# Out projection stage of a hybrid backbone layer: direction sums accumulated in PSUM, second norm on ScalarE, routing by pairs of tiles

## The chip, the cores and the metric

One NeuronCore of a Trainium2 chip runs the whole layer in one launch. The metric is device time in microseconds of one execution. PE is the matrix engine (TensorE), DVE is VectorE, ACT is ScalarE, POOL is GpSimd, and SP is the engine whose queue starts most transfers. SBUF is the on-chip memory of 128 partitions; PSUM holds the matmuls' results in eight banks, of which ACT and DVE read.

## What is computed

The reference is one layer over 2048 latent tokens of width 1024 and 256 tokens of context. An input projection feeds three mixers that run over the sequence in both directions (SSD, RWKV-7, GLA). Their normed outputs are concatenated, projected, added to the residual and normed; a second norm gives the input of a mixture of 64 experts, top 8, with one shared expert. In the part that the change touches, for each token:

```
y_ssd  = rmsnorm_groups((fwd + flip(bwd) + D*xs) * silu(z), ssd_norm_w)
y_rwkv = (groupnorm(fwd + flip(bwd)) * lnx_w + lnx_b + bonus) * gate
y_gla  = rmsnorm_groups(fwd + flip(bwd), gla_norm_w) * silu(og)
mix = concat([y_ssd, y_rwkv, y_gla]) @ w_out
x = layernorm(DN_ALPHA * x + g1 * mix, ln1_w, ln1_b)
h = layernorm(x) * (1.0 + sc2) + sh2
scores = sigmoid(h @ router_w)
sel = scores + router_b
top_g = top_k(sum of the best two sel of each of 8 groups, 4)
idx = top_k(sel where the group is in top_g, 8)
wts = scores[idx] / sum(scores[idx]) * 2.5
x = layernorm(DN_ALPHA * x + g2 * moe(h, idx, wts), ln2_w, ln2_b)
```

## The kernel before

The stage around the change is a loop over 16 tiles of 128 latent tokens, c from 17 down to 2 (the GLA and SSD backward scans take their last steps in it), between the scans and the experts:

```
for c in range(17,1,-1):
    ym=mid.mix(c,pm,y17 if c==17 else X.pass2(c),G.pass2(c))
    f=mid.proj(c,pm,mp,ym)
    rt.tile(c,mp,f,mid.rw)
```

X.pass2 (lines 906 to 920) finishes the SSD: two matmuls of the carried state with the loaded C (L916) into one PSUM bank, on DVE the decay product (L918), the sum with the forward part sy (L919), and the two steps of the next state hb (L903, L904). G.pass2 (L1111 to L1119) does the same for GLA: one matmul (L1117), one add of the forward part on DVE (L1118), one state step (L1108). mix (L1176 to L1213) turns the RWKV backward rows around with a matmul by the reversal matrix (L1189), adds the forward rows on DVE (L1190), takes sums and squares per head on ACT (L1193, L1197, L1198, L1200), a Newton rsqrt of ten columns on DVE (the helper of L35 to L44), scales on ACT (L1207 to L1209), and leaves the concatenated tile ym of 128 x 1024 (L1210 to L1212).

proj (L1231 to L1262) transposes ym by eight matmuls with the identity (L1237) and splits it into a high and a low part (yTh on ACT L1239, yTl on DVE L1240). Two groups of 24 matmuls of 128 x 512 (L1248: high by high, high by low, low by high) give the projection; each group ends in a DVE residual with row sums (L1249). The first norm `ln` (square on ACT L1220, affine steps on DVE L1221 and L1230, ten one-column DVE steps between) gives x; the second, with perm=True, gives the hidden tile m_h with its columns reordered (DVE L1221 and L1229). m_h is stored (L1254), transposed by eight matmuls into the banks a0 and a1 (L1258), copied by ACT (hTf, L1259) and stored (L1260).

rt.tile (L1281 to L1322) does the routing of one tile: eight router matmuls (L1287), exp on ACT (L1288), some 25 small DVE instructions for sigmoid, group limit, top 8 and weights, a matmul with a triangle U and one with ones that give each token's rank within its expert (L1312), and the slots (L1313 to L1322). rt.scatter later issues 128 indirect transfers on POOL (L1328) that enter tokens into the experts' lists.

PSUM tiles have names, and a name has a fixed number of buffers: `g` and `mm` two each, c0, c1, a0 and a1 one each. With one buffer, the next user of a name waits, in program order, until the last reader of the one before is done. Before the change c0 serves X.pass2, G.pass2 and mix, c1 the router and the ranks, a0 and a1 the hidden transposes. The order of instructions on each engine is set when the program is built, by a scheduler that moves instructions ahead of others as far as data and buffers allow; an engine then works through its list in order. The loads and stores of the stage all go through SP's queue.

Behind the loop come the experts: the shared expert on the first 8 tiles (up matmuls L1512), the scatter, then the routed experts.

Of the kernel before, what the change touches and what calls it, by code (L numbers as in the profile page):

```python
# [1127 lines left out]
class Mid:  # L1128
# [50 lines left out]
    def mix(s, c, pool, ys, yg):  # L1179

        nc=s.nc; l=c-2; S=s.S; r0=l*128
        ld=lambda n,src,w: (lambda t:(nc.sync.dma_start(t,src),t)[1])(pool.tile([128,w],F32,name=n,bufs=2))
# [4 lines left out]
        ym=pool.tile([128,1024],F32,name='m_ym',bufs=2)
        p=s.ps.tile([128,256],F32,name='c0',bufs=1)
        nc.tensor.matmul(p,S['rev'],yb,start=True,stop=True)  # L1189
        nc.vector.tensor_tensor(yf,p,yf,op=OP.add)  # L1190
# [6 lines left out]
        for h in range(4): nc.scalar.activation(yr[:,h*64:h*64+64],yf[:,h*64:h*64+64],AF.Square,bias=nm[:,h:h+1],accum_out=st[:,2+h:3+h])  # L1197
# [66 lines left out]
class Route:  # L1264
# [14 lines left out]
        nc.sync.dma_start(S['tab'].rearrange("(p s) c->p (s c)",p=128),tb)  # L1279
        s.slot=f([128,16,8],'q_slot',I32); s.tk=f([128,16],'q_tk',I32)  # L1280
    def tile(s, c, pool, f, rw):  # L1281
        nc=s.nc; r0=(c-2)*128
# [8 lines left out]
        sel=t([128,8,8],'sel'); sf=sel.rearrange("p a b->p (a b)")
        nc.vector.tensor_tensor(sf,sc,s.rb,op=OP.add)
        top=t([128,8,8],'top')
        for g in range(8): nc.vector.max(top[:,g],sel[:,g])
        gs=t([128,8],'gs'); nc.vector.tensor_tensor(gs,top[:,:,0],top[:,:,1],op=OP.add)
# [12 lines left out]
        w=t([128,64],'w'); nc.vector.tensor_scalar(w,sc,n,2.5,op0=OP.mult,op1=OP.mult)
        nc.sync.dma_start(s.S['h'][r0:r0+128,1024:1088],w)

        q=p[:,128:256]
        nc.tensor.matmul(q,s.U,two(M),start=True,stop=False); nc.tensor.matmul(q,s.on,two(s.cum),start=False,stop=True)  # L1312
        sl=t([128,64],'sl'); nc.vector.tensor_tensor(sl,p[:,128:192],s.e0,op=OP.add)  # L1313
# [544 lines left out]
```

## Time and profile before

| | |
|---|---|
| median of 3 runs | 3917.51 us (3916.85 to 3926.28) |
| the profiled execution | 3949.18 us, its span 3947.4 us |
| granted PE clock over the span | 0.943 |
| PE busy | 3525.1 us, 89% of the span |
| DVE busy | 2685.3 us, 68% |
| ACT busy | 1706.2 us, 43% |
| POOL busy | 1329.0 us, 34% |
| DMA | 745.81 MB, mean 189 GB/s |
| 1600 to 1900 us (end of the scans): PE, DVE, ACT busy | 227.62, 207.66, 133.19 of 300 us, clock 0.83 |
| 1900 to 2260 us (the tile stage) | 312.54, 319.08, 193.26 of 360 us, clock 0.94 |
| 2260 to 3947 us (the experts) | 1574.80, 1080.30, 603.65 of 1687 us, clock 0.97 |

Busy time is the time in which an engine executes instructions, so an engine that waits within its list is not busy. The granted clock is the TensorE clock as a share of full speed. A table by stage says more than the page's shares of the whole span, because the stages have different limits.

### The profile page before, as it was taken

Reading aid. Unit: us, or ns where it says so; the run is one execution under the profiler, and the core shown is the slowest. Engines: PE = TensorE matmul, PEld = TensorE weight load, DVE = VectorE, ACT = ScalarE, POOL = GpSimd, SP = SyncE. Lnnn points to the kernel's source line nnn. Section 1 sums busy time; section 2 is a strip of 40 time slices with the busy share of each in tenths; the row PEclk is TensorE's granted clock in tenths of the full one; section 3 lists DMA queues with packets and bytes.
Section 4 is the critical chain, followed back from the end, with each engine's and each line's share of the span. In section 5 each row is a group of like instructions: output and inputs, shape, how many; then the busy total and the mean of one; then the engine's idle time right before and its main releaser. Section 6 shows DMA issues by size and latency. Waiting matters only on the chain. (4 is left out here: it accounts for less than half of the span.)

```text
span 3947.4 us, 66654 instructions
## 1 busy us (share of the span) xinstructions
PE 3525.1 (89%) x23502; PEld 3006.8 (76%) x23502; DVE 2685.3 (68%) x6775; ACT 1706.2 (43%) x3955; POOL 1329.0 (34%) x1224
## 2 busy tenths in 40 slices
PE   8989887999799978995789899999999999999986
PEld 5978777888688857774567678888888887787865
DVE  4576865876777648775899766666666665666658
ACT  3555553545454533444555323343333333333334
POOL 0243543443343310100044533333334343344323
PEclk9999989999899988996899899999999999999988
DMA  7656554333333276864665468788788887888874
GB/s 228 212 184 206 175 152 133 83 100 101 111 92 98 51 223 215 250 186 167 199 194 167 156 172 231 220 251 243 219 241 242 251 235 227 245 242 229 254 210 160
DMA packets 498511, 745.81 MB, mean 189 GB/s; under 512 B 156704, under 2 KB 393312, under 8 KB 469216
## 3 DMA queue, kind: packets, MB, share of 16 engines
q1 hardware_dynamic: 438880, 522.20, 41.0%
q0 software_dynamic: 59296, 219.33, 22.0%
q8 instruction: 187, 3.06, 0.3%
q14 instruction: 148, 1.21, 0.1%
HBM read 524.31 MB, written 217.06 MB: 188 GB/s over the span
## 5 line engine op out<-in xcount | busy, mean ns | idle before, releaser
L1546 POOL DMA_INDIRECT d_f<-yo,en x162 | 346.6, 2140 | 569.4 <-DVE yo L1543 314.0
L1543 DVE SCALAR_TENSOR_TENSOR yo<-mm,f_w,g2r 128x512 f32<-128x512 f32 (+7 forms) x324 | 236.6, 744 | 265.6 <-PE mm L1541 171.2
L1562 POOL DMA_INDIRECT xg<-d_h,en x162 | 232.1, 1433 | 371.8 <-DVE yo L1543 61.6
L184 PE MATMUL b<-uh,wh 128*128 128x384 f32 (+1 forms) x912 | 320.1, 356 | 12.6 <-ACT sce L805 5.2
L184 PE MATMUL b<-ul,wh 128*128 128x384 f32 (+1 forms) x912 | 320.3, 352 | 5.9 <-DMA ul<-d_ul 3.6
L184 PE MATMUL b<-uh,wl 128*128 128x384 f32 (+1 forms) x912 | 320.9, 352 | 0.0
L1445 DVE TENSOR_TENSOR w13l<-raw,w13h 128x2048 fp32r<-128x2048 f32 x102 | 232.8, 2283 | 25.3 <-ACT w13h L1445 25.3
L1445 ACT ACTIVATE w13h<-raw 128x2048 fp32r<-128x2048 f32 x102 | 195.0, 1914 | 104.5 <-DMA raw<-in_exp_w_dram 94.4
L1328 POOL DMA_INDIRECT d_tab<-q_tk,q_slot x128 | 146.9, 1148 | 248.2 <-DVE q_slot L1321 135.7
L1541 PE MATMUL mm<-w2h,hWh 128*128 128x512 f32 (+7 forms) x480 | 202.3, 422 | 13.0 <-DVE yo L1543 12.3
L1512 PE MATMUL a<-w13h,xTh 128*128 128x512 f32 x464 | 190.2, 410 | 9.0 <-ACT xTh L1471 8.4
L1445 DVE TENSOR_TENSOR w2l<-raw,w2h 128x2048 fp32r<-128x2048 f32 x66 | 151.3, 2293 | 68.9 <-ACT w2h L1445 66.0
L1512 PE MATMUL a<-w13l,xTh 128*128 128x512 f32 x464 | 190.4, 410 | 8.0 <-DVE w13l L1445 8.0
L1541 PE MATMUL mm<-w2h,hWl 128*128 128x512 f32 (+7 forms) x480 | 186.9, 404 | 6.8 <-DVE hWl L1504 6.8
L1541 PE MATMUL mm<-w2l,hWh 128*128 128x512 f32 (+7 forms) x480 | 191.2, 399 | 1.6 <-DVE w2l L1445 1.6
L184 PEld LDWEIGHTS b<-uh,wh 128*128 128x128 f32 x912 | 175.9, 194 | 20.2 <-ACT sce L805 6.4
L1512 PE MATMUL a<-w13h,xTl 128*128 128x512 f32 x464 | 187.7, 405 | 0.0
L184 PEld LDWEIGHTS b<-ul,wh 128*128 128x128 f32 x912 | 177.7, 195 | 9.3 <-DVE ul L139 4.0
L184 PEld LDWEIGHTS b<-uh,wl 128*128 128x128 f32 x912 | 177.6, 195 | 1.4
L1445 ACT ACTIVATE w2h<-raw 128x2048 fp32r<-128x2048 f32 x66 | 126.5, 1916 | 116.1 <-DMA raw<-in_exp_w_dram 70.5
L1475 PE MATMUL g<-ident,xg 128*128 128x128 f32 (+9 forms) x1296 | 167.6, 263 | 9.9 <-DMA xg<-d_h,en 5.8
L1475 PEld LDWEIGHTS g<-ident,xg 128*128 128x128 f32 (+9 forms) x1296 | 142.4, 140 | 38.2 <-issue 14.6
(706 smaller groups left out, 10553.8 us busy)
## 6 DMA issues: line engine op xcount, KB each, us to landing
raw<-in_exp_w_dram SPq DMA_DIRECT2D x162, 1024.0 KB
w13h<-in_exp_w_dram SPq DMA_DIRECT2D x30, 1024.0 KB
wr<-in_w_in_dram SPq DMA_DIRECT2D x46, 512.0 KB
uht<-d_uh POOLq DMA_DIRECT2D x32, 512.0 KB
ult<-d_ul POOLq DMA_DIRECT2D x32, 512.0 KB
mrw<-in_ada_w_dram SPq DMA_DIRECT2D x32, 512.0 KB
rkX<-d_ops SPq DMA_DIRECT2D x36, 384.0 KB
rpx<-d_rw SPq DMA_DIRECT2D x54, 192.0 KB
```

The lines of the kernel that those rows point to most:

```text
L184: s.nc.tensor.matmul(P.rearrange("p (i t)->p i t",t=128),l,r[:,a//128:,k],start=(i==0),stop=(i==23)); i+=1
L1328: d=s.nc.gpsimd.indirect_dma_start(out=s.S['tab'],out_offset=bass.IndirectOffsetOnAxis(ap=s.slot[:,l,k:k+1],axis=0),in_=s.tk[:,l:l+1],in_o ...
L1445: pin(nc.scalar.activation(H,r,AF.Copy)); pin(nc.vector.tensor_tensor(L,r,rnd(H),op=OP.subtract))
L1475: for k in range(4): nc.tensor.transpose(p[:,k,:m],B['x'][:m,(4*g+k)*128:(4*g+k+1)*128],s.id[:m,:m])
L1512: nc.tensor.matmul(p,a[:,k],b[:,:,k],start=(i==0),stop=(i==23)); i+=1
L1541: nc.tensor.matmul(r[:m],a[:,k],b[:,k,cs],start=(i==0),stop=(i==5)); i+=1
L1543: else: nc.vector.scalar_tensor_tensor(o[:m,cs],r[:m],B['w'] if isinstance(B['w'],float) else B['w'][:m],s.g2[:m,cs],op0=OP.mult,op1=OP.mult)
L1546: d=nc.gpsimd.indirect_dma_start(out=s.S['f'],out_offset=bass.IndirectOffsetOnAxis(ap=B['en'][:m],axis=0),in_=o[:m],in_offset=None,compute ...
L1562: s.nc.gpsimd.indirect_dma_start(out=x[:m],out_offset=None,in_=s.S['h'],in_offset=bass.IndirectOffsetOnAxis(ap=B['en'][:m],axis=0))
```

## The change

Four edits, all in the stage described. (1) The forward parts of GLA and RWKV are no longer added on DVE: a second matmul with the identity accumulates them in PSUM, and ACT reads the sums from there. The bank that G.pass2 hands to mix (now c1) and mix's own (c0) are therefore held until the scalings at mix's end. (2) In the second norm the two wide DVE steps, one of them with reordered output, are replaced by one small DVE product, one ACT pass that normalises and reorders, and two wide DVE steps on contiguous rows; the modulation rows are reordered once, ahead of the stage. (3) Routing handles two tiles at a time: an odd tile only leaves its exp in half of a shared buffer, and the even tile after it runs the chain for both. (4) PSUM names move: X.pass2 writes a1 (before c0), G.pass2 c1 (before c0), the router a0 and the ranks a0 and a1 (before c1).

```diff
@@ G.pass2 @@
-        po=s.ps.tile([128,256],F32,name='c0',bufs=1)
-        nc.tensor.matmul(po,qb,Sb,start=True,stop=True)
-        nc.vector.tensor_tensor(y,po,y,op=OP.add)
-        return y
+        po=s.ps.tile([128,256],F32,name='c1',bufs=1)
+        nc.tensor.matmul(po,qb,Sb,start=True,stop=False)
+        nc.tensor.matmul(po,s.id,y,start=False,stop=True)
+        return po
@@ modrow @@
+        t=rowb(s.nc,pool,s.S['mod'][1024*v:1024*v+1024],1024,'mtmp' if perm else name)
+        if not perm: return t
+        o=pool.tile([128,1024],F32,name=name)
+        s.nc.scalar.activation(o.rearrange("t (k p)->t k p",k=8),t.rearrange("t (p k)->t k p",k=8),AF.Copy); return o
@@ mix @@
-        nc.tensor.matmul(p,S['rev'],yb,start=True,stop=True)
-        nc.vector.tensor_tensor(yf,p,yf,op=OP.add)
+        nc.tensor.matmul(p,S['rev'],yb,start=True,stop=False)
+        nc.tensor.matmul(p,s.id,yf,start=False,stop=True)
...
-        for h in range(4): nc.scalar.activation(yr[:,h*64:h*64+64],yf[:,h*64:h*64+64],AF.Copy,accum_out=nm[:,h:h+1])
+        for h in range(4): nc.scalar.activation(yr[:,h*64:h*64+64],p[:,h*64:h*64+64],AF.Copy,accum_out=nm[:,h:h+1])
...
-        for h in range(4): nc.scalar.activation(yf[:,h*64:h*64+64],yf[:,h*64:h*64+64],AF.Identity,bias=nb[:,h:h+1],scale=rs[:,2+h:3+h])
+        for h in range(4): nc.scalar.activation(yf[:,h*64:h*64+64],p[:,h*64:h*64+64],AF.Identity,bias=nb[:,h:h+1],scale=rs[:,2+h:3+h])
...
-        for h in range(4): nc.scalar.activation(yg[:,h*64:h*64+64],yg[:,h*64:h*64+64],AF.Copy,scale=rs[:,6+h:7+h])
-        nc.vector.tensor_tensor(ym[:,768:1024],yg,og,op=OP.mult)
+        for h in range(4): nc.scalar.activation(ym[:,768+h*64:832+h*64],yg[:,h*64:h*64+64],AF.Copy,scale=rs[:,6+h:7+h])
+        nc.vector.tensor_tensor(ym[:,768:1024],ym[:,768:1024],og,op=OP.mult)
@@ ln @@
-        nc.vector.scalar_tensor_tensor(u,x,ve[:,0:1],w,op0=OP.add,op1=OP.mult)
+        if not perm: nc.vector.scalar_tensor_tensor(u,x,ve[:,0:1],w,op0=OP.add,op1=OP.mult)
...
-            nc.vector.scalar_tensor_tensor(o,v(u),rs,v(b),op0=OP.mult,op1=OP.add)
+            nc.vector.tensor_tensor(ve[:,0:1],ve[:,0:1],rs,op=OP.mult)
+            nc.scalar.activation(u.rearrange("t (k p)->t k p",k=8),x.rearrange("t (p k)->t k p",k=8),AF.Identity,bias=ve[:,0:1],scale=rs)
+            nc.vector.tensor_tensor(u,u,w,op=OP.mult); nc.vector.tensor_tensor(out,u,b,op=OP.add)
@@ Route.tile @@
-        p=s.ps.tile([128,512],F32,name='c1',bufs=1)
+        p=s.ps.tile([128,128],F32,name='a0',bufs=1)
...
+        if l%2: s.sc=t([128,2,64],'sc')
+        sc=s.sc; nc.scalar.activation(sc[:,l%2],p[:,0:64],AF.Exp,scale=-1.0)
+        if l%2: return
...
+        for j in (1,0):
+            q=s.ps.tile([128,128],F32,name=f'a{1-j}',bufs=1)
+            nc.tensor.matmul(q,s.U,two(M[:,j]),start=True,stop=False); nc.tensor.matmul(q,s.on,two(s.cum),start=False,stop=bool(j))
+            if not j: nc.tensor.matmul(q,s.on,two(M[:,1]),start=False,stop=True)
+            nc.vector.tensor_tensor(sl[:,j],q[:,0:64],s.e0,op=OP.add)
...
@@ the stage @@
-                X.ps=G.ps=ps; X.bank='c0'; G.pool=tp.enter_context(P('p2g',side='right'))
+                X.ps=G.ps=ps; X.bank='a1'; G.pool=tp.enter_context(P('p2g',side='right'))
-                mid.sh2=mid.modrow(mw,1,'sh2r'); mid.sc2=mid.modrow(mw,2,'sc2r')
+                mid.sh2=mid.modrow(mw,1,'sh2r',True); mid.sc2=mid.modrow(mw,2,'sc2r',True)
```

The lines of the changed kernel stand some 3 to 15 further down: L1248 is L1251 there, L1258 is L1261, L1287 is L1291.

The order of instructions moves on PE. In these rows `mm` is the projection's PSUM tile, `a_..` a0 or a1, `c_..` c0 or c1, `g` the transposes of ym, and x4 stands for four equal instructions. Before, around the hidden transposes of tile 13, the fifth of the loop:

```order
L1248 MATMUL mm<-woh,yTl 128x512
L1117 MATMUL c_22893<-gSb_20326,gq_22889 128x256
L1258 MATMUL a_21997<-ident,m_h 128x128 x4
L1258 MATMUL a_22003<-ident,m_h 128x128 x4
L1189 MATMUL c_22909<-m_yb,rev 128x256
L1312 MATMUL c_21742<-q_M,q_U 128x128
L1312 MATMUL c_21742<-q_cum,q_on 128x128
L916 MATMUL c_23148<-hb_20316,sC_23144 128x256 x2
L1287 MATMUL c_22010<-rtw,hTf 128x128 x8
L1117 MATMUL c_23161<-gSb_20327,gq_23157 128x256
L1189 MATMUL c_23177<-m_yb,rev 128x256
L1237 MATMUL g<-ident,m_ym 128x128 x8
```

These stand behind the projection matmuls of seven tiles (17 to 11): two more than its own and those ahead of it. After, around the hidden transposes of tile 15:

```order
L1251 MATMUL mm<-woh,yTl 128x512
L1261 MATMUL a_21446<-ident,m_h 128x128 x4
L1261 MATMUL a_21452<-ident,m_h 128x128 x4
L1291 MATMUL a_21459<-rtw,hTf 128x128 x8
L916 MATMUL a_21478<-hb_20316,sC_21474 128x256 x2
L1192 MATMUL c_21799<-m_yb,rev 128x256
L1193 MATMUL c_21799<-m_yf,ident 128x256
L1117 MATMUL c_21783<-gSb_20326,gq_21779 128x256
L1118 MATMUL c_21783<-gy_21781,ident 128x256
L1240 MATMUL g<-ident,m_ym 128x128 x8
L1251 MATMUL mm<-woh,yTh 128x512
L1251 MATMUL mm<-wol,yTh 128x512
```

They stand behind the matmuls of three tiles, 17 to 15: the last set in front of them is the tile's own, and the next set (14's) comes behind the router, X.pass2 and the sums. So it is in all 16 tiles.

On ACT, before, where copies of one tile (yTh), statistics of a second and third, and norm passes of others alternate:

```order
L1239 ACTIVATE yTh<-g 128x512 x2
L1198 ACTIVATE m_ym,m_st<-gy_22355 128x64 x4
L1200 ACTIVATE m_z,m_st<-so_22347 128x256 x2
L1193 ACTIVATE m_ym,m_nm<-m_yf 128x64 x4
L1197 ACTIVATE m_ym,m_st<-m_yf,m_nm 128x64 x4
L1208 ACTIVATE m_ym<-so_22079,m_rsy 128x256 x2
L1209 ACTIVATE gy_22087<-gy_22087,m_rsy 128x64 x3
L1220 ACTIVATE m_h,l2e<-m_x,l2e 128x1024
L1207 ACTIVATE m_yf<-m_yf,m_nb,m_rsy 128x64 x4
L1209 ACTIVATE gy_22087<-gy_22087,m_rsy 128x64
L1239 ACTIVATE yTh<-g 128x512 x2
L1220 ACTIVATE m_h,l1e<-m_xt,l1e 128x1024
```

These are pieces of at least three tiles. After, around the norms of tile 15:

```order
L1242 ACTIVATE yTh<-g 128x512 x2
L1223 ACTIVATE m_h,l1e<-m_xt,l1e 128x1024
L1223 ACTIVATE m_h,l2e<-m_x,l2e 128x1024
L1231 ACTIVATE m_xt<-m_x,l2e,l2y 128x1024
L1262 ACTIVATE hTf<-a_21446 128x512
L1262 ACTIVATE hTf<-a_21452 128x512
L1293 ACTIVATE q_sc<-a_21459 128x64
L1203 ACTIVATE m_z,m_st<-so_21481 128x256 x2
L1211 ACTIVATE m_ym<-so_21481,m_rsy 128x256 x2
L1212 ACTIVATE m_ym<-c_21491,m_rsy 128x64 x3
L1210 ACTIVATE m_yf<-c_21507,m_nb,m_rsy 128x64 x4
L1212 ACTIVATE m_ym<-c_21491,m_rsy 128x64
```

The two norm squares (L1223), the reordering pass (L1231), the hidden copies (L1262) and the exp (L1293) of one tile now follow each other, then the mix of the next tile (L1203 to L1212).

On SP, before, around the two stores of a tile's hidden state (d_h, d_hT):

```order
L1254 DMA d_h<-m_h 128x1024
L1114 DMA gq_23961<-gqb 128x128
L1107 DMA gbs<-gstb 128x256
L1260 DMA d_hT<-hTf 128x1024
L1182 DMA m_yb<-d_yb 128x256
L911 DMA sC_24216<-ssdC 128x2x128
```

Two loads of later GLA steps stand between the stores, and the load of C (sC) is one of several behind them. After, around the same stores of tile 15:

```order
L1257 DMA d_h<-m_h 128x1024
L1263 DMA d_hT<-hTf 128x1024
L911 DMA sC_22504<-ssdC 128x2x128
L913 DMA sy_22506<-d_ys 128x512
L902 DMA sbs<-stb 128x512
```

The loads that X.pass2 and the mix of the next tile need (sC, sy, sbs, m_z) now stand directly behind the store d_hT.

## Rows read from the trace of the kernel before

**Rows 1.** Windows ahead of and in the tile stage: stretch, length, engines' busy us, PEclk, DMA share, GB/s
```profile
1880.00:1904.00 24.00, 13.43 (x29) 7.58 (x30) 15.91 (x63) 14.74 (x80) 0.00 (x0) 0.50 0.92 288
1904.00:2210.00 306.00, 272.68 (x1360) 224.96 (x1360) 279.62 (x1276) 172.61 (x661) 111.23 (x96) 0.96 0.54 172
```

**Rows 2.** Timeline of TensorE: start us, us, instruction, [idle before it <-releaser]
```profile
1884.88 2.07 PE L916 MATMUL c<-hb,sC 128*128 128x256 f32 x4 [0.52 <-DVE m_yf L1190]
...
1903.34 0.99 PE L1248 MATMUL mm<-woh,yTh 128*128 128x512 f32 x1
...
1905.81 0.39 PE L1248 MATMUL mm<-woh,yTh 128*128 128x512 f32 x1
...
1915.37 0.40 PE L1248 MATMUL mm<-woh,yTl 128*128 128x512 f32 x1
1915.61 1.03 PE L1237 MATMUL g<-ident,m_ym 128*128 128x128 f32 x8
...
2225.21 3.78 PE L1287 MATMUL c<-rtw,hTf 128*128 128x128 f32 x16 [0.32 <-issue]
2229.74 1.94 PE L1258 MATMUL a<-ident,m_h 128*128 128x128 f32 x8 [0.74 <-DVE q_r L1316]
...
2256.18 0.38 PE L1312 MATMUL c<-q_M,q_U 128*128 128x128 f32 x2
```

**Rows 3.** Groups by line, 1870 to 2262: xcount | busy us, mean ns | idle before, releaser
```profile
L1229 DVE SCALAR_TENSOR_TENSOR m_h<-m_xt,l2y,sh2r 128x1024 f32<-128x1024 f32 x16 | 32.5, 2033 | 0.4 <-DVE q_M L1304 0.3
...
L1197 ACT ACTIVATE m_ym<-m_yf,m_nm 128x64 f32<-128x64 f32 x64 | 21.5, 338 | 15.3 <-DVE m_nm L1194 12.8 <-DVE gy L1118 1.6 <-DVE q_sl L1314 0.5
...
L1221 DVE SCALAR_TENSOR_TENSOR m_xt<-m_x,l2e,sc2r 128x1024 f32<-128x1024 f32 x16 | 20.3, 1271 | 0.0
...
L1198 ACT ACTIVATE m_ym<-gy 128x64 f32<-128x64 f32 x64 | 15.6, 247 | 24.2 <-DVE gy L1118 14.2 <-DMA m_yb<-d_yb 9.6 <-DVE m_rst L39 0.4
...
L1118 DVE TENSOR_TENSOR gy<-c,gy 128x256 f32<-128x256 f32 x16 | 6.6, 414 | 3.9 <-DMA gy<-d_yg 1.9 <-remote 1.0 <-PE c L1117 0.9
```

**Rows 4.** Timeline of VectorE: a mix, a norm, a route
```profile
1887.19 0.48 DVE L1108 SCALAR_TENSOR_TENSOR gSb<-gSb,gdecb,gbs 128x256 f32<-128x256 f32 x1 [1.06 <-DMA gbs<-gstb]
1887.59 0.68 DVE L918 TENSOR_TENSOR so<-c,sdea 128x512 f32<-128x512 f32 x1
1888.19 0.68 DVE L903 TENSOR_TENSOR hb<-hb,sddec 128x512 f32<-128x512 f32 x1
...
2207.98 0.16 DVE L44 SCALAR_TENSOR_TENSOR l2y<-l2t,l2y 128x1 f32<-128x1 f32 x1
2208.18 2.07 DVE L1229 SCALAR_TENSOR_TENSOR m_h<-m_xt,l2y,sh2r 128x1024 f32<-128x1024 f32 x1
2210.24 0.69 DVE L1249 SCALAR_TENSOR_TENSOR m_xt<-m_x,mm 128x512 f32<-128x512 f32 x1
...
2248.26 0.53 DVE L1290 RECIPROCAL q_sc<-q_sc 128x64 f32<-128x64 f32 x1
...
2251.61 0.25 DVE L1304 TENSOR_TENSOR q_M<-q_M,q_sel 128x64 f32<-128x64 f32 x1
```

**Rows 5.** Timeline of ScalarE: a mix, a norm, the hidden copies
```profile
1884.86 0.26 ACT L1193 ACTIVATE m_ym<-m_yf 128x64 f32<-128x64 f32 x1 [0.71 <-DVE m_yf L1190]
...
1886.16 0.35 ACT L1197 ACTIVATE m_ym<-m_yf,m_nm 128x64 f32<-128x64 f32 x1 [0.24 <-DVE m_nm L1194]
...
1894.49 0.91 ACT L1208 ACTIVATE m_ym<-so,m_rsy 128x256 f32<-128x256 f32 x2 [1.09 <-DVE m_rsy L44]
...
1896.02 1.42 ACT L1207 ACTIVATE m_yf<-m_yf,m_nb,m_rsy 128x64 f32<-128x64 f32 x4
...
2211.62 1.14 ACT L1220 ACTIVATE m_h<-m_xt,l1e 128x1024 f32<-128x1024 f32 x1
...
2231.71 0.60 ACT L1259 ACTIVATE hTf<-a 128x512 f32<-128x512 f32 x1 [0.25 <-PE a L1258]
```

**Rows 6.** Timeline of SP's queue: the issue of the load used at 1887.19
```profile
1882.18 0.43 SPq L1107 DMA_DIRECT2D gbs<-gstb  x1
```

More of the change, by code (lines that the diff above doesn't have):

```diff
@@ L1188, in mix @@
         p=s.ps.tile([128,256],F32,name='c0',bufs=1)
[L1189 to L1190 removed]
+        nc.tensor.matmul(p,S['rev'],yb,start=True,stop=False)
+        nc.tensor.matmul(p,s.id,yf,start=False,stop=True)
         nm=pool.tile([128,4],F32,name='m_nm',bufs=2)
         yr=ym[:,512:768]
[L1193 removed]
+        for h in range(4): nc.scalar.activation(yr[:,h*64:h*64+64],p[:,h*64:h*64+64],AF.Copy,accum_out=nm[:,h:h+1])
         nc.vector.tensor_scalar(nm,nm,-1.0/64,None,op0=OP.mult)
         st=pool.tile([128,10],F32,name='m_st',bufs=2)
[L1197 removed]
+        for h in range(4): nc.scalar.activation(yr[:,h*64:h*64+64],p[:,h*64:h*64+64],AF.Square,bias=nm[:,h:h+1],accum_out=st[:,2+h:3+h])
         for h in range(4): nc.scalar.activation(ym[:,h*64:h*64+64],yg[:,h*64:h*64+64],AF.Square,accum_out=st[:,6+h:7+h])
@@ L1281, in tile @@
     def tile(s, c, pool, f, rw):
-        nc=s.nc; r0=(c-2)*128
+        nc=s.nc; l=c-2; r0=l*128
         t=lambda shape,n,dt=F32,b=2: pool.tile(shape,dt,name='q_'+n,bufs=b)
-        p=s.ps.tile([128,512],F32,name='c1',bufs=1)
+        p=s.ps.tile([128,128],F32,name='a0',bufs=1)
         two=lambda x: x[:,None].to_broadcast([128,2,64])
-        for k in range(8): nc.tensor.matmul(p[:,0:128],f[:,k],two(rw[:,k]),start=(k==0),stop=(k==7))
-        sc=t([128,64],'sc'); nc.scalar.activation(sc,p[:,0:64],AF.Exp,scale=-1.0)
+        for k in range(8): nc.tensor.matmul(p,f[:,k],two(rw[:,k]),start=(k==0),stop=(k==7))
@@ L1289, in tile @@
+        if l%2: s.sc=t([128,2,64],'sc')
+        sc=s.sc; nc.scalar.activation(sc[:,l%2],p[:,0:64],AF.Exp,scale=-1.0)
+        if l%2: return
         nc.vector.tensor_scalar(sc,sc,1.0,None,op0=OP.add)
         nc.vector.reciprocal(sc,sc)
[L1291 to L1295, printed above, removed]
@@ L1297, in tile @@
-        g8=t([128,8],'g8'); nc.vector.max(g8,gs); nc.vector.memset(g8[:,4:8],3e38)
-        gm=t([128,8],'gm'); nc.vector.match_replace(gm,g8,gs,-3e38)
+        sel=t([128,2,8,8],'sel'); sf=sel.rearrange("p j a b->p j (a b)")
+        nc.vector.tensor_tensor(sf,sc,two(s.rb),op=OP.add)
+        top=t([128,2,8,8],'top')
+        for j in range(2):
+            for g in range(8): nc.vector.max(top[:,j,g],sel[:,j,g])
+        gs=t([128,2,8],'gs'); nc.vector.tensor_tensor(gs,top[:,:,:,0],top[:,:,:,1],op=OP.add)
@@ L1299, in tile @@
+        g8=t([128,2,8],'g8')
+        for j in range(2): nc.vector.max(g8[:,j],gs[:,j])
+        nc.vector.memset(g8[:,:,4:8],3e38)
+        gm=t([128,2,8],'gm')
+        for j in range(2): nc.vector.match_replace(gm[:,j],g8[:,j],gs[:,j],-3e38)
         nc.vector.tensor_tensor(gm,gm,gs,op=OP.is_equal)
-        nc.vector.scalar_tensor_tensor(sel,gm[:,:,None].to_broadcast([128,8,8]),-1e30,sel,op0=OP.mult,op1=OP.add)
-        t8=t([128,8],'t8'); nc.vector.max(t8,sf)
-        M=t([128,64],'M'); n=t([128,1],'n')
@@ L1303, in tile @@
-        nc.vector.match_replace(M,t8,sf,-3e38)
+        nc.vector.scalar_tensor_tensor(sel.rearrange("p j a b->p (j a) b"),gm.rearrange("p j a->p (j a)")[:,:,None].to_broadcast([128,16,8]),-1e30,sel.rearrange("p j a b->p (j a) b"),op0=OP.mult,op1=OP.add)
+        t8=t([128,2,8],'t8'); M=t([128,2,64],'M'); n=t([128,2],'n')
+        for j in range(2): nc.vector.max(t8[:,j],sf[:,j])
+        for j in range(2): nc.vector.match_replace(M[:,j],t8[:,j],sf[:,j],-3e38)
         nc.vector.tensor_tensor(M,M,sf,op=OP.not_equal)
-        nc.vector.scalar_tensor_tensor(sc,sc,1.0,M,op0=OP.mult,op1=OP.mult,accum_out=n)
+        for j in range(2): nc.vector.scalar_tensor_tensor(sc[:,j],sc[:,j],1.0,M[:,j],op0=OP.mult,op1=OP.mult,accum_out=n[:,j:j+1])
@@ L1307, in tile @@
         nc.vector.reciprocal(n,n)
[L1308 to L1313, printed above, removed]
+        w=t([128,2,64],'w')
+        for j in range(2): nc.vector.tensor_scalar(w[:,j],sc[:,j],n[:,j:j+1],2.5,op0=OP.mult,op1=OP.mult)
@@ L1314, in tile @@
+        nc.sync.dma_start(s.S['h'][r0:r0+256,1024:1088].rearrange("(j p) c->p j c",j=2),w)
+        sl=t([128,2,64],'sl')
+        for j in (1,0):
[3 more added lines that the diff above has]
+            nc.vector.tensor_tensor(sl[:,j],q[:,0:64],s.e0,op=OP.add)
         nc.vector.tensor_tensor(sl,sl,M,op=OP.mult)
-        nc.vector.tensor_tensor(s.cum,s.cum,M,op=OP.add)
@@ L1316, in tile @@
-        r=t([128,8],'r'); nc.vector.max(r,sl)
-        l=c-2; ix=s.slot[:,l]; j=t([128,2,8],'ix',I32)
+        for j in (1,0): nc.vector.tensor_tensor(s.cum,s.cum,M[:,j],op=OP.add)
+        r=t([128,2,8],'r')
+        for j in range(2): nc.vector.max(r[:,j],sl[:,j])
+        ix=s.slot[:,l:l+2]; x=t([128,2,2,8],'ix',I32)
         nc.vector.tensor_scalar(ix,r,-1.0,None,op0=OP.add)
-        nc.vector.tensor_scalar(j[:,0],ix,127,None,op0=OP.bitwise_and)
-        nc.vector.tensor_scalar(j[:,1],ix,7,None,op0=OP.logical_shift_right)
@@ L1321, in tile @@
-        nc.vector.scalar_tensor_tensor(ix,j[:,0],1040.0,j[:,1],op0=OP.mult,op1=OP.add)
-        nc.vector.tensor_scalar(s.tk[:,l:l+1],s.tok,float(r0),None,op0=OP.add)
+        nc.vector.tensor_scalar(x[:,0],ix,127,None,op0=OP.bitwise_and)
+        nc.vector.tensor_scalar(x[:,1],ix,7,None,op0=OP.logical_shift_right)
+        nc.vector.scalar_tensor_tensor(ix,x[:,0],1040.0,x[:,1],op0=OP.mult,op1=OP.add)
+        for j in range(2): nc.vector.tensor_scalar(s.tk[:,l+j:l+j+1],s.tok,float(r0+128*j),None,op0=OP.add)
```

5 lines of the change are left out of this document (1 added, 4 removed).

## The prediction, made before the changed kernel ran

> **What bounds the kernel now.** The stage's busy times come first [rows 1]. In its main stretch VectorE (DVE) works 279.6 of 306 us (91%), TensorE (PE) 272.7 (89%), ScalarE (ACT) 172.6 (56%), and PE has a granted clock of 0.96. In the 24 us before it the mixes of the first tiles come one after another: PE is busy 13.4 of 24 us, and the granted clock is 0.50, the 1.2 GHz level against 2.4 GHz later. The stage lasts from the first projection matmul at 1903.34 to the last routing matmuls at 2256.18 [rows 2]: 352.9 us, 22 per tile. Both engines can be that full only because the tiles overlap: PE's order of before (shown with the change) has seven sets of 48 projection matmuls ahead of the hidden transposes of the fifth tile (13). While a tile goes through its norms, PE already does the next ones. DVE is the fuller engine; the two direction adds (0.41 each, 16 of either) and the second norm's two wide passes (1.27 and 2.03) [rows 3] are its work.
>
> **The change part by part.** *The order.* X.pass2's output moves to bank a1, which the hidden transposes use too, and each of these banks has one buffer. So X.pass2 of tile c-1 may write a1 only after tile c's hidden state has been through it. That closes a ring: 48 matmuls of tile c, first norm, second norm, hidden transposes, copies, router, X.pass2 of c-1, its mix, transposes, 48 matmuls of c-1. PE's order after the change shows just this: the hidden transposes of a tile stand right behind its own 48 matmuls, in all 16 tiles (1, 2, 3 to 16 sets, where before it was 3, 3, 4, 5, 7 up to 16). ACT's order agrees: no norm pass of another tile stands between those of one. A step of the ring that another tile used to cover now costs its full length. I add up those lengths.
>
> (a) 48 matmuls, 12.3: from 1903.34 to the next instruction at 1915.61, after a stretch with PE half idle, which is what the ring has before each set [rows 2].
>
> (b) Both norms, 13.2. The last half's residual, mean and square 2.6 (0.69 DVE, 0.2 small, 1.14 plus accumulator read on ACT, hops); then ten dependent one-column steps at 0.195 (the next begins 0.20 after L44's last one) = 1.95; the wide affine step, 1.3 like L1221. Second norm: mean and square 1.5, ten steps 1.95, the new product 0.2, the new ACT pass 1.2 (as wide as the square; its permuted read may cost up to 0.7 more), two wide DVE products 2.5 (two of L1221's 1.27) [rows 3 to 5].
>
> (c) Hidden transposes and copies 2.6 (2229.74 to the second copy's end at 2232.31), eight router matmuls 1.9 (half of the 3.78 for sixteen), hops 0.3: 4.8 [rows 2, 5].
>
> (d) X.pass2's two matmuls 2.1 [rows 2], after a wait for C. Its load stands behind the 512 KB store of the hidden state on SP's queue. A load behind such a transfer came 5.0 us after its issue (issued 1882.18, used 1887.19) [rows 4, 6]; transposes' copies to router end cover 2 to 5 of that. Bounds 0 and 2.5, taken 1.2, the middle, as nothing in the rows decides.
>
> (e) Five DVE passes of 512 wide at 0.62 from start to start (1887.59 to 1888.19 for the first, hops) 3.1, two ACT squares 0.9 like the two L1208, ten rsqrt steps 2.0, ACT's scalings up to the last that reads c0, nine of ten, 3.0 (from 1894.49 the first nine take 2.9): 9.0 [rows 4, 5].
>
> (f) Bank c0 is now read by ACT up to those scalings, so the sums for tile c-2 (two matmuls, 2.1) start only then, and ACT's order has their statistics ahead of tile c-1's yTh copies: sums and mean 1.3 (1884.86 to 1886.16), four squares at 0.34 1.3, four GLA squares at 0.25 1.0, then the two copies at 0.60 and a hop 1.3: 7.0 [rows 3, 5].
>
> A tile without routing: 12.3 + 13.2 + 4.8 + 1.2 + 2.1 + 9.0 + 7.0 = 49.6.
>
> *Routing.* Every second tile now carries the chain for two, and it stands ahead of X.pass2's DVE step. Exp with its hops 0.5; the chain from reciprocal to mask took 3.6 for one tile (2248.26 to 2251.86) [rows 4], and the doubled top-k instructions and widths add 2.0, so 5.6; ten PE passes at the lower clock 2.5; the last add 0.3; less 0.7 of the wait for C that this hides: +8.2, hence 57.8. The slot arithmetic behind it lies under X.pass2's matmuls.
>
> *The small edits.* The DVE adds that go [rows 3] are no step of the ring; the identity matmuls that replace them are, inside the 2.1 of (f). The permuted copies of the two rows run once on ACT, a microsecond or so each, before the stage. The scatter's last issues grow to a pair of tiles, sixteen instead of eight; the shared expert's second product stands far behind and covers them. If that cover were gone it would be some 10 us.
>
> *Behind the stage.* Before, 91 of the shared expert's matmuls run ahead of the last routing matmuls; after the change all stand behind. At 0.23 each (42 steps from 1905.81 to 1915.37 [rows 2]) that is 21.
>
> **The sum.** 8 × 49.6 + 8 × 57.8 = 859; the last tile has no next mix (d's matmuls, e, f): −18, so 841 against 352.9: +488; with the 21, **+509**. The profiled execution took 3949.2 (span 3947.4), so its like would take about 4458. The median of the runs, 3917.5, lies 31.7 lower; on that scale **4427 us**.
>
> Bounds. With PE at the upper clock throughout, (a) is 11.0 (48 × 0.228), transposes 1.0 (1915.61; at the lower one 1.9), router 1.0, each pair of 256-wide matmuls 1.05, passes 1.25; with C never waited for: 6.4 per tile and 1.2 per pair less, 110 in all: 4317. With C at 2.5 (+21), the permuted read dear (+11) and a hop of 0.1 more at some twenty places of each tile (+32): 4491.
>
> The clock is the largest of these. The row is [rows 1]: PE 56% busy at 0.50, 89% busy at 0.96; the ring leaves PE some 22 of 50 us busy, so nearer to the first. I take the lower level outside the 48 matmuls.
>
> The Trainium skill (Perfetto Trace Analysis, Optimizing Scalar/DVE Operations) gives ScalarE a fixed cost per instruction of about 93 ns on SBUF and 51 ns on PSUM. By that the 20 ACT reads that move to PSUM would each be 42 ns shorter, as an estimate 0.8 per tile or 13 in all, and the sum 4414; no row of before shows the pair side by side.
>
> **The rivals.**
>
> R1, faster: DVE's relief decides. The wide passes fall from 3.3 to 2.7 and the adds go (0.83) [rows 3]; taking two tiles at a time saves perhaps 0.45 per tile in fixed parts of small instructions: 1.9 × 16 = 30 on an engine that is 91% busy, so 3888. It decides as long as PE still has another tile's matmuls to do while the norms run. For it speaks DVE's share [rows 1]; against it that after the change no such matmul stands there in any tile, and engines work in order. 2%. The Trainium skill says in the same section that a saturated DVE may be relieved by handing work to Scalar, which is this rival's rule; in Optimizing Tensor Performance, Matmuls, it says that independent matmul groups should rotate through different PSUM banks, which X.pass2 in a1 offends. The order shown with the change sides with the second.
>
> R2, the clock stays up: PE's 22 busy us per tile are bunched, and it rises within the sets anyway (the 48 of the row take 12.3, and 11.0 would be the pace of its end [rows 2]). If it stays up between them: 4317 to about 4370. Against it stands the 0.50 of the first 24 us [rows 1]. 15%.
>
> R3, only half a ring: the norms stay hidden, only the mix is serial, as when a1 comes free earlier than I read it. 13.2 × 16 = 211 less: 4216. 4%.
>
> R4, longer than all bounds: SP's queue, where the loads for the mix now stand behind both stores of a tile, delays each mix by more than 2.5. One more full landing of 5.0 per tile is 80: 4507. 6%.
>
> R5, the change does nothing: the routing, the adds and the order cancel, within 0.3% (12 us, about what a measurement of this kernel can tell from no change). 1%.
>
> **How the numbers follow.** The forecast (4370 to 4491, with the sum 4427) has 72%, R2 15%, R4 6%, R3 4%, R1 2%, R5 1%. The range takes in the forecast and most of R2 and leaves R1, R3, R4 and R5 out: 4330 to 4491. Faster by over 0.3%: 2%; within: 1%; slower: 97%.
>
> **What would show it.** The stage's last routing matmuls should come about 841 us after its first projection matmul instead of 352.9. PE should be idle for about 13 us in front of each tile's hidden transposes, released by DVE's h, and for about 9 between X.pass2 and the direction sums; DVE and ACT should be busy half the time or less there, and the granted clock well under 0.96. The experts' stage should be as long as before. I am wrong if PE does one tile's matmuls while another tile is in its norms, if the stage is under 650 us, or if the waits in front of the hidden transposes are under 8 us; and wrong in the reason, if the stage is long but PE waits for transfers in it.

## The result and the profile after

The changed kernel takes 4414.4 us (median of 4 runs, 4406.6 to 4421.2) against 3921.9 for the kernel before: 1.1255 of before, 95% interval 1.1226 to 1.1285. The forecast was 4427, with 4330 to 4491 as its range.

The windows of the changed kernel, of the tile stage and of the experts behind it (columns as in [rows 1]):

```profile
1898.00:2711.00 813.00, 376.14 (x1525) 306.62 (x1526) 357.02 (x1312) 220.20 (x710) 113.46 (x112) 0.72 0.23 78
2711.00:4407.00 1696.00, 1588.60 (x8598) 1352.92 (x8596) 1087.29 (x1921) 609.34 (x825) 645.20 (x363) 0.98 0.77 226
```

The stage ends at 2710.8, 812.6 us after its first projection matmul, where it took 353. In [rows 1] DVE was busy 91% and PE 89%; here it is 44% and 46%, and the granted clock is 0.72 instead of 0.96. No engine is near its limit. TensorE's timeline of one tile shows why (the rows answer to [rows 2]):

```profile
1898.19 0.50 PE L1251 MATMUL mm<-woh,yTh 128*128 128x512 f32 x1 [1.72 <-ACT yTh L1242]
...
1909.03 0.39 PE L1251 MATMUL mm<-woh,yTl 128*128 128x512 f32 x1
1923.39 1.97 PE L1261 MATMUL a<-ident,m_h 128*128 128x128 f32 x8 [13.97 <-DVE m_h L1232]
1925.19 3.78 PE L1291 MATMUL a<-rtw,hTf 128*128 128x128 f32 x16
1928.76 1.47 PE L916 MATMUL a<-hb,sC 128*128 128x256 f32 x4
1939.14 1.22 PE L1192 MATMUL c<-m_yb,rev 128*128 128x256 f32 x2 [8.91 <-ACT m_yf L1210]
...
1945.56 0.50 PE L1251 MATMUL mm<-woh,yTh 128*128 128x512 f32 x1 [1.52 <-ACT yTh L1242]
```

The last of the 48 matmuls starts at 1909.03, and PE stands for 13.97 us until DVE has the hidden tile. Then transposes, router and X.pass2 follow without a gap, PE stands 8.91 us until ScalarE's scalings free c0, and the next set starts at 1945.56: 47.4 us after the one before. No projection matmul or norm of another tile lies between. The waits of the whole stage (total, times, longest) say that this is so in every tile:

```profile
PE a L1261 <- DVE m_h L1232: 230.9, 16, 20.6
...
PE c L1192 <- ACT m_yf L1210: 125.2, 14, 9.1
```

16 waits of 14.4 us on average ahead of the hidden transposes and 14 of 8.9 ahead of the sums: 356 us of idle PE, where the kernel before had 11 at the same two places.

### The profile page after: what moved, and what is told of

Read it like the earlier page. It is cut to its first block, busy times and chain, and to the rows that moved or that the text cites. A ratio compares the mean times of both kernels' runs of the same rounds, so it can differ in the third digit from the quotient of the medians.

```text
span 4407.3 us, 66708 instructions
## 1 busy us (share of the span) xinstructions
PE 3602.9 (82%) x23582; PEld 3075.9 (70%) x23582; DVE 2725.1 (62%) x6647; ACT 1741.4 (40%) x3973; POOL 1311.0 (30%) x1224
## 5 line engine op out<-in xcount | busy, mean ns | idle before, releaser
L1343 POOL DMA_INDIRECT d_tab<-q_tk,q_slot x128 | 130.3, 1018 | 727.3 <-DVE q_slot L1336 690.8
L1261 PE MATMUL a<-ident,m_h 128*128 128x128 f32 x128 | 31.3, 426 | 230.9 <-DVE m_h L1232 230.9
L1556 PE MATMUL mm<-w2h,hWh 128*128 128x512 f32 (+7 forms) x480 | 201.4, 420 | 12.6 <-DVE yo L1558 11.8
L1261 PEld LDWEIGHTS a<-ident,m_h 128*128 128x128 f32 x128 | 25.1, 223 | 237.4 <-issue 122.2
```

The source lines that it names most:

```text
L1261: for k in range(4): nc.tensor.transpose(p[:,k],h[:,(4*g+k)*128:(4*g+k+1)*128],s.id)
L1343: d=s.nc.gpsimd.indirect_dma_start(out=s.S['tab'],out_offset=bass.IndirectOffsetOnAxis(ap=s.slot[:,l,k:k+1],axis=0),in_=s.tk[:,l:l+1],in_o ...
L1556: nc.tensor.matmul(r[:m],a[:,k],b[:,k,cs],start=(i==0),stop=(i==5)); i+=1
```

## The experiments

Ratios are to the kernel before on the same chip. "Stage" is the time from the first projection matmul to the last routing matmul in the run's profile, "experts" what comes behind. The profile of before that the prediction used took 3949.2, 27 above the median of 3921.9, so a few tens of us between two profiles prove nothing; below 1% the ratios decide.

| run | ratio to before (95%) | stage | experts |
|---|---|---|---|
| before | 1 | 353 | 1691 |
| the change | 1.1255 (1.1226 to 1.1285) | 813 | 1697 |
| 1 before, X.pass2 in a1 | 1.0937 (1.0894 to 1.0981) | 713 | 1689 |
| 2 change, X.pass2 in c0 | 1.0208 (1.0166 to 1.0249) | 397 | 1721 |
| 3 change, X.pass2 in c1 | 1.0193 (1.0140 to 1.0246) | 391 | 1723 |
| 4 change, X.pass2 in g | 1.0250 (1.0202 to 1.0297) | 423 | 1705 |
| 5 as 2, without the sums | 1.0061 (1.0040 to 1.0082) | 346 | 1704 |
| 6 as 2, without the new norm | 1.0045 (1.0030 to 1.0059) | 345 | 1709 |
| 7 as 2, without the pairs | 1.0045 (1.0032 to 1.0059) | 353 | 1691 |
| 8 before, new norm alone | 1.0089 (1.0061 to 1.0118) | 371 | 1689 |
| 9 change, old norm | 1.1142 (1.1114 to 1.1170) | 765 | 1704 |
| 10 before, sums alone | 0.9996 (0.9979 to 1.0012) | 342 | 1683 |
| 11 before, pairs alone | 1.0041 (1.0026 to 1.0057) | 333 | 1708 |
| 12 before, sums taken out at once | 0.9991 (0.9975 to 1.0006) | 333 | 1690 |

**Runs 1 to 4: which bank makes the ring.** Run 1 is the kernel before with one name changed; runs 2 to 4 are the change with another bank for X.pass2 (in run 4 without bufs=1, as g has two buffers).

```diff
-                X.ps=G.ps=ps; X.bank='c0'; G.pool=tp.enter_context(P('p2g',side='right'))
+                X.ps=G.ps=ps; X.bank='a1'; G.pool=tp.enter_context(P('p2g',side='right'))
```

> The kernel before with one word changed: X.pass2 writes bank a1. Theory (the ring comes from the shared bank): the tile stage becomes serial, with the old norm, the old adds and the old routing as its steps. Against the ring of the change (47.4 us a tile without routing) the second norm is about 2.9 shorter, and the statistics no longer wait for the scalings of the tile before, about 3.2 shorter: some 41 to 46 us a tile, stage 660 to 740 us instead of 353, time 4200 to 4310. Rival (the ring comes from the direction sums that hold c0 and c1, and from the longer norm): those are absent here, so the stage stays within 60 us of 353, time under 3980.

> The change with X.pass2 back in bank c0 and everything else kept. Theory (shared bank): PE's order runs one to two sets ahead again, the stage is 330 to 400 us, time 3880 to 3970; if DVE's relief counts it is the low end, if the direction sums' longer hold of c0 and ScalarE's reordering pass of 2.2 us count it is the high end. Rival (the sums' hold and the longer norm make the ring): the stage stays over 600 us, time over 4150.

> The change with X.pass2 in bank c1, which G.pass2's sum also uses and holds until the scalings. Theory: no bank of the hidden transposes is shared, so the norms are hidden behind the next tile's matmuls; but X.pass2 of a tile now waits for the scalings of the tile before. PE's order is one set ahead instead of zero: stage 350 to 480 us, time 3910 to 4050, above the run with c0. Rival: as for c0, over 4150.

> The change with X.pass2 in the two buffers named g, which the transposes of the concatenated tile use, so that neither the hidden transposes' banks nor c0 and c1 are shared. Theory: one set ahead, stage 350 to 480 us, time 3910 to 4050. Rival (any single-buffer reuse is enough, whatever the bank): as long as the change, 4380 to 4440.

One word costs 9.4%: 368 of the change's 492 us. TensorE's timeline of run 1 has the ring, with the old norm as a shorter wait (10.9 us ahead of the hidden transposes):

```profile
1917.21 1.94 PE L1258 MATMUL a<-ident,m_h 128*128 128x128 f32 x8 [10.93 <-DVE m_h L1229]
...
1921.67 1.03 PE L916 MATMUL a<-hb,sC 128*128 128x256 f32 x4
...
1934.09 1.97 PE L1237 MATMUL g<-ident,m_ym 128*128 128x128 f32 x8 [4.09 <-DVE m_ym L1212]
```

Sets of 48 start at 1892.6, 1936.7 and 1980.1: 44 us a tile. The rival fell: without any direction sum in PSUM and with the old norm the ring stands. Runs 2 to 4 take the shared bank out of the change and are 1.9 to 2.5% above before instead of 12.6%; in run 2, where the bank is the only difference, that gives back 10.5%, 411 us. The order there has the hidden transposes of the first tiles behind 2.08, 3.54, 5 and 6 sets (c0), 2, 3, 4 and 5 (c1, g, but for fractions). Run 2 takes 4018, over my high end for it (3970). Runs 3 (4013) and 4 (4034) lie within their ranges, but run 3 is not above run 2, as I had expected. In run 4 PE still waits 52.4 us in all for the hidden tile, in front of the hidden transposes of five tiles. So freeing a1 does not bring back the kernel before.

**Runs 5 to 8: what remains.** Runs 5 to 7 each take one of the three parts out of run 2, run 8 puts one into the kernel before. The code of the part is that of before (or of the change, in run 8); run 7 keeps the router's tile in a0:

```diff
-        p=s.ps.tile([128,512],F32,name='c1',bufs=1)
+        p=s.ps.tile([128,512],F32,name='a0',bufs=1)
```

> The change with X.pass2 and G.pass2 in c0 and the direction sums back on DVE; the new norm and the pairs stay. Three theories on what still makes the change slower once the ring is gone (2.1% with bank c0). A, the sums hold c0 and c1 from the first matmul to the scalings, so only one mix can be under way: then this run is the one that falls, to 0.990 to 1.006 of before. B, the second norm's chain with ScalarE's reordering pass: this run stays at 1.012 to 1.025. C, the pairs: this run stays at 1.012 to 1.025.

> The change with X.pass2 in c0 and the second norm as before; sums and pairs stay. A: 1.012 to 1.025 of before. B: 0.990 to 1.006. C: 1.012 to 1.025.

> The change with X.pass2 in c0 and one tile routed at a time (its PSUM tile in a0); sums and new norm stay. A: 1.010 to 1.020 of before. B: 1.010 to 1.020. C: 0.990 to 1.006, and shared-expert matmuls run ahead of the last routing matmuls again.

> The kernel before with the second norm's new form alone. A and C: DVE does 0.8 us less per tile (3.30 against 2 times 1.23), so 0.995 to 1.000 of before. B: ScalarE's strided pass of 2.2 us lengthens each tile, 1.005 to 1.020.

None of A, B and C held alone: any two parts together cost 0.45 to 0.61%, all three 2.1%. A second, smaller ring, on c0, would be one reason. ScalarE's last scalings of a tile (L1210) in run 2, then PE's X.pass2 of the next (L916), at two of the tiles:

```profile
2000.89 1.30 ACT L1210 ACTIVATE m_yf<-c,m_nb,m_rsy 128x64 f32<-128x64 f32 x4
...
2047.85 0.72 ACT L1210 ACTIVATE m_yf<-c,m_nb,m_rsy 128x64 f32<-128x64 f32 x2
```

```profile
2002.24 1.13 PE L916 MATMUL c<-hb,sC 128*128 128x256 f32 x4 [1.42 <-issue]
...
2049.38 1.02 PE L916 MATMUL c<-hb,sC 128*128 128x256 f32 x4
```

The scalings end at 2002.19, and X.pass2 starts at 2002.24; in the other pair it comes 0.8 us after. At 11 of 14 tiles of run 2 it starts within 1.3 us of the moment c0 comes free. But so it does, within 2 us, at 12 of 14 tiles of run 7, and in run 2 PE hardly waits at that point. The window of run 2 to the last projection matmul, and its waits in front of X.pass2:

```profile
1894.44:2247.90 353.46, 293.17 (x1437) 239.43 (x1436) 266.87 (x1172) 200.08 (x707) 93.05 (x90) 0.93 0.47 153
```

```profile
PE c L916 <- issue: 2.4, 3, 1.4
...
PE c L916 <- ACT m_yf L1210: 0.2, 1, 0.2
```

PE is idle for 60.3 us of this window (before: 33.3; runs 5 to 7: 23 to 30), and 2.6 of them lie in front of X.pass2. More lies in front of the transposes of ym (17.0) and of the projection matmuls (22.6), which come later in a tile. X.pass2 recurs every 22.8 us in run 2 (1905.7 to 2202.0, 13 times), every 20.3, 19.9 and 19.6 us in runs 6, 7 and 10, which also hold c0 for the sums, and every 20.5 us in the kernel before, which does not. From 1982.0 on, tiles of 27 to 35 us take turns in run 2 with tiles of 18 to 23, which fits the pairs' chain. So that the hold of c0 is what makes the three parts cost more together is not shown, and which wait does it was not tried.

Run 8 shows how a part can lose without any ring. Windows of run 8 (to the last projection matmul, to the last routing matmul, experts):

```profile
1911.00:2211.00 300.00, 267.27 (x1332) 218.40 (x1331) 263.88 (x1232) 205.68 (x677) 89.44 (x81) 0.97 0.54 175
2211.00:2282.00 71.00, 43.92 (x209) 37.07 (x207) 49.55 (x210) 21.47 (x30) 40.63 (x38) 0.78 0.44 158
2282.00:3971.00 1689.00, 1578.12 (x8502) 1343.28 (x8502) 1080.71 (x1911) 603.71 (x817) 640.06 (x357) 0.97 0.78 226
```

The ratio lies in B's range, but the stretch of the tiles is shorter and not longer: 300 us from 307, with DVE at 88%. What grew is the tail: five router groups now stand behind the last set, where before had three (2211.36, 2225.21 and 2244.36), and the tail takes 71 us where before took 47 (the row is shown at run 11). So I read it as the order of the instructions, and not the time of one of them, that took the gain; no run tries the order alone. The new norm alone costs more (0.89%) than together with the sums (run 7, 0.45%, with the router in another bank): the parts do not add.

**Run 9: the length of the ring, step by step.** The change with the second norm's old lines and unpermuted rows.

> The change with bank a1 and the second norm as before. If every step of the ring costs its full length, the stage shrinks by what the new form adds between the last Newton step and the hidden tile: 4.94 us (18.39 to 23.33 in the first tile) against 2.05 for the old step, 2.9 a tile, 46 in all; the ratio falls from 1.1255 to 1.112 to 1.116. If something beside the ring paces the tiles (SP's queue, the transfers, the clock), it falls by less than half of that, to 1.120 or more.

1.1142: 44 us less of before's 3926, and the stage 47 shorter. The new norm's steps cost their full length in the ring, as reckoned. SP's queue and the transfers pace nothing there: in this trace, too, no step of the ring waits for a DMA.

**Runs 10 to 12: parts alone, and a version that might win.** Run 10 is the sums, run 11 the pairs on the kernel before, run 12 this (and the same for GLA, with one copy of 256 columns):

```diff
-        nc.tensor.matmul(p,S['rev'],yb,start=True,stop=True)
-        nc.vector.tensor_tensor(yf,p,yf,op=OP.add)
+        nc.tensor.matmul(p,S['rev'],yb,start=True,stop=False)
+        nc.tensor.matmul(p,s.id,yf,start=False,stop=True)
+        yf=pool.tile([128,256],F32,name='m_y2',bufs=2)
...
-        for h in range(4): nc.scalar.activation(yr[:,h*64:h*64+64],yf[:,h*64:h*64+64],AF.Copy,accum_out=nm[:,h:h+1])
+        for h in range(4): nc.scalar.activation(yf[:,h*64:h*64+64],p[:,h*64:h*64+64],AF.Copy,accum_out=nm[:,h:h+1])
```

> The kernel before with the direction sums alone, read from PSUM up to the scalings as in the change (mix and X.pass2 in c0, G.pass2 in c1, the router in a0). If the hold of c0 and c1 costs by itself: 1.008 to 1.020 of before. If it only costs together with the new norm and the pairs: 0.994 to 1.005.

> The kernel before with routing by pairs alone (ranks in a0 and a1 as in the change). All shared-expert matmuls then stand behind the last routing matmuls; in the two runs with pairs and without the ring the experts' stage was 14 and 19 us longer, the tile stage 7 and 9 shorter: 1.002 to 1.008 of before. If the pairs are free by themselves: 0.995 to 1.001.

> A version that may beat both: the kernel before with both direction sums in PSUM, but ScalarE takes them out at once (its first pass over the RWKV sum writes SBUF, one more pass of 256 copies the GLA sum), so c0 is held no longer than before and no name moves. DVE does 0.83 us less per tile, PE 0.87 more, ScalarE 0.4 more. If DVE (91%) sets the pace: 0.993 to 0.998. If PE (89%) takes over as the bound: 0.999 to 1.005.

The sums alone cost nothing and win nothing, so the hold of the banks has no price by itself. The pairs alone cost 0.4%, within the expected range. Their windows show the give-back (to the last projection matmul, to the last routing matmul, experts):

```profile
1904.00:2203.00 299.00, 269.17 (x1396) 221.23 (x1395) 279.98 (x1211) 173.57 (x666) 112.57 (x90) 0.99 0.55 178
2203.00:2237.00 34.00, 11.66 (x66) 10.58 (x64) 26.20 (x92) 12.72 (x15) 27.16 (x23) 0.66 0.72 258
2237.00:3945.00 1708.00, 1600.10 (x8599) 1362.09 (x8598) 1088.17 (x1923) 608.84 (x825) 650.17 (x363) 0.97 0.77 225
```

The same tail in the kernel before:

```profile
2210.00:2257.00 47.00, 35.50 (x174) 29.72 (x174) 35.43 (x143) 16.05 (x21) 26.24 (x24) 0.82 0.57 215
```

It shrinks from 47 us to 34, but PE has 11.7 us of work in it instead of 35.5: the shared expert's matmuls that filled it use a0 and a1, which the pairs' ranks now use too, so they stand behind (92 ahead of the last routing matmul before, 1 in run 11), and the experts' stage grows from 1691 to 1708. That the shared banks put them there is read from the order. The windows do not add up to the 0.4% either: the stage is 20 shorter and the experts 17 longer, and the 16 us of the ratio are less than what two profiles can tell. Run 12 is not distinguishable from before (0.9991; its interval includes 1 and overlaps both expectations). No version here beats the kernel before.

## Why the prediction was right, point by point

*The ring* held, and is shown: the order forecast it, the timeline has it in all 16 tiles, run 1 makes it with one name, run 2 undoes it. Rivals R1, R3 and R5 fell by the result itself (4414 against 3888, 4216 and no change). R4's price, a landing of 5 us per mix, is not there: the only waits for a DMA on the engines of the ring are 5.5 us of ScalarE's, for loads of the shared expert. The Trainium skill's rule on rotating PSUM banks (Perfetto Trace Analysis, Optimizing Tensor Performance) pointed the right way; run 1 prices its breach here at 44 us a tile against 22. Its advice on handing a saturated DVE's work to Scalar (Optimizing Scalar/DVE Operations) did not pay here: run 8 is 0.9% slower.

*The terms*, in the tile of the rows above and the next one:

| step | forecast | measured |
|---|---|---|
| a 48 matmuls | 12.3 | 11.2 (1898.19 to 1909.42) |
| b both norms | 13.2 | 14.0 (to 1923.39) |
| c, d transposes, router, wait for C, X.pass2 | 8.1 | 6.9 (to 1930.27) |
| e DVE steps, rsqrt, scalings | 9.0 | 8.9 (to 1939.14) |
| f sums, statistics, copies | 7.0 | 6.4 (to 1945.56) |
| a tile | 49.6 | 47.4 |
| more with routing | 8.2 | 8.5 (55.9 from 1945.56 to 2001.43) |

Over the first fourteen tiles, a tile without routing takes 46.6 on average and one with routing 56.7: 10.0 more, against the 8.2 of the forecast.

(a) I took the slow start from [rows 2] for every set; in this tile the first matmul takes 0.50. Eleven of the 16 sets take 11.2, as here; five take 12.7 to 12.8, among them the one at 2001.43, whose first matmul takes 0.79.

(b) was too short by ScalarE's reordering pass: 1.2 forecast, at most 1.9, measured 2.2. VectorE's timeline from the last Newton step to the hidden tile, and ScalarE's pass:

```profile
1918.20 0.16 DVE L44 SCALAR_TENSOR_TENSOR l2y<-l2t,l2y 128x1 f32<-128x1 f32 x1
...
1920.84 1.23 DVE L1232 TENSOR_TENSOR m_xt<-m_xt,sc2r 128x1024 f32<-128x1024 f32 x1 [2.29 <-ACT m_xt L1231]
1922.10 1.23 DVE L1232 TENSOR_TENSOR m_h<-m_xt,sh2r 128x1024 f32<-128x1024 f32 x1
```

```profile
L1231 ACT ACTIVATE m_xt<-m_x,l2e,l2y 128x1024 f32<-128x1024 f32 x16 | 35.6, 2225 | 32.2 <-DVE l2e L1230 32.2
```

The pass with permuted read takes 2225 ns for the same 128 x 1024 elements that the square reads in 1.14 us [rows 5]. It is the read and not the function: the reordering of a modulation row ahead of the stage, a plain copy with the same stride, takes as long.

```profile
L1161 ACT ACTIVATE sh2r<-mtmp x1: 2080/2080/2080, 1828.0 to 1828.0; 128x1024 f32<-128x1024 f32 x1
```

The Trainium skill (SBUF — State Buffer, Door 1) says that fp32 reads may step up to four elements before each costs a new 16-byte line; this one steps eight, and the two times agree with a penalty. I had not weighed that rule.

(e) and (f) answer the estimate from the Trainium skill (Perfetto Trace Analysis, Optimizing Scalar/DVE Operations), 42 ns less for each ScalarE read that moves from SBUF to PSUM. The GLA squares of one tile before and of one after, from start to start:

```profile
1890.84 0.24 ACT L1198 ACTIVATE m_ym<-gy 128x64 f32<-128x64 f32 x1
...
1891.08 0.24 ACT L1198 ACTIVATE m_ym<-gy 128x64 f32<-128x64 f32 x1
```

```profile
1943.79 0.24 ACT L1201 ACTIVATE m_ym<-c 128x64 f32<-128x64 f32 x1
...
1943.99 0.25 ACT L1201 ACTIVATE m_ym<-c 128x64 f32<-128x64 f32 x1
```

The length of one does not change, but the next starts sooner: by the median, 239 ns become 197 here and for the sums (L1196) and GLA scalings (L1212), 332 become 289 for the squares with bias (L1200) and 331 become 290 for the scalings L1210. That is 41 to 43 ns in all five groups, so the trace agrees. My sum went without it; in (f), twelve such reads make up most of the 0.6 by which it came out shorter.

(c) and (d) held several errors that partly cancel. I read "x16" of the router as two tiles; it is one tile's eight matmuls in sixteen records, so the router takes 3.6 at the lower clock (1925.19 to 1928.76), not 1.9; the 1.0 in my low bound has the same error. It starts 1.8 after the first hidden transpose, where I had 2.9 with both copies and hops: ScalarE still copies the second half then. And C is never waited for. SP's timeline:

```profile
1926.02 0.32 SPq L1263 DMA_DIRECT2D d_hT<-hTf  x1
1930.27 0.37 SPq L911 DMA_DIRECT2D sC<-ssdC  x1
```

The load of C stands right behind the store, as the order said, but it starts at 1930.27, when X.pass2 has just released the buffer: with two buffers it is the load of one tile later, and has a whole tile's time to land. I had taken the place in the order for the time of need.

*Routing*: the chain came out as summed. TensorE's timeline of the second tile:

```profile
1970.86 1.94 PE L1261 MATMUL a<-ident,m_h 128*128 128x128 f32 x8 [14.06 <-DVE m_h L1232]
1972.63 2.70 PE L1291 MATMUL a<-rtw,hTf 128*128 128x128 f32 x16
1981.20 0.77 PE L1325 MATMUL a<-q_M,q_U 128*128 128x128 f32 x2 [5.87 <-DVE q_M L1314]
...
1983.04 0.64 PE L1326 MATMUL a<-q_M,q_on 128*128 128x128 f32 x2
1983.99 2.08 PE L916 MATMUL a<-hb,sC 128*128 128x256 f32 x4 [0.32 <-DVE q_sl L1327]
1995.01 1.22 PE L1192 MATMUL c<-m_yb,rev 128*128 128x256 f32 x2 [8.95 <-ACT m_yf L1210]
...
2001.43 0.79 PE L1251 MATMUL mm<-woh,yTh 128*128 128x512 f32 x1 [2.13 <-ACT yTh L1242]
```

5.9 us of PE's wait for the mask (6.1 forecast for exp and chain), 2.5 for ten passes, 0.3 for the last add: 8.7. The 0.7 that I took off for the wait for C was not there to hide. Of the 1.3 that are left of the 10.0, 0.7 lie in X.pass2, which takes 1.8 on average in tiles with routing and 1.1 in the others.

*The clock*: 0.72 over the stage. I had taken the lower level for all that lies outside the sets. The hidden transposes kept to it in all 16 tiles (1.94 or 1.97, as in [rows 2]). The router, X.pass2 and the transposes of ym did not. Router and X.pass2 of a later tile:

```profile
2341.32 2.68 PE L1291 MATMUL a<-rtw,hTf 128*128 128x128 f32 x16
2343.84 1.03 PE L916 MATMUL a<-hb,sC 128*128 128x256 f32 x4
```

The router takes 3.78 once and 2.6 to 3.6 in the other tiles (at 2211.36 of the kernel before, in the stretch at 0.96, it took 1.95). X.pass2 takes 1.03, half of the 2.07 of [rows 2], in 7 of 15 tiles, and the transposes of ym take from 1.04 to 1.97, between the two lengths of [rows 2]. So R2 came in part: in these tiles the clock rose within the router, and most sets have no slow start. But it was not up all through the ring, and the time lies above R2's 4317 to 4370.

*Behind the stage* I forecast 21 for the 91 matmuls that move behind; the experts took 5.9 more (1696.5 against 1690.6). My own list of signs had said that they would take as long as before, which did not go with the 21 in the sum. PE's busy time there grew by 12 and its idle time shrank by 7. In runs 2 to 6 and 11, which have the pairs but no ring, they took 14 to 32 more.

*The sum*: the stage 813 against 841 forecast, the experts +6 against +21. The two profiled executions differ by 460, the medians by 492; the forecast was +509. Where the 32 us between the two measures lie, in an execution of before that was slower than its others, the profiles don't say. So the mechanism and its price were right, but that 4427 came within 0.3% of 4414 is in part luck: on the profiled executions, from which the terms were read, the forecast is 49 too long, and errors of both signs cancel in the ring.

## What to carry to other kernels

A single-buffered PSUM name is an edge in the program's order: before moving a tile to another bank, ask which long chain that bank's last user hangs on, and count how many tiles' work the order still has in front of that chain. Where the order shows none, add the chain's steps at full length; that gave the stage's length within 4% here, and swapping one name back is the cheapest experiment. A relief of the busiest engine is worth nothing if the tail behind the loop or the work that filled it moves the other way.

## What the runs showed that I had not expected

ScalarE reading with a stride of eight elements and writing in order takes 2225 ns for 128 x 1024, against 1.14 us for the same width in order [rows 5]. The same small ScalarE pass follows the one before it 41 to 43 ns sooner when it reads PSUM instead of SBUF, though its recorded length hardly changes. Three parts that cost 0.45 to 0.61% two by two cost 2.1% together; which wait makes the difference stays open.
